# A macaron block's mixer woven by estimated engine clocks, with weight slots of its own for each dense stream and a full-array recurrence

## The chip, the core and the metric

The kernel runs on one core of a Trainium2 chip. Its time is the device time of one execution in microseconds; the lower the better. PE is the matrix engine (TensorE), DVE the vector engine, ACT the scalar engine, POOL the general engine (GpSimd), SP the engine that issues most transfers.

## What is computed

One layer of a hybrid model on 1024 tokens of width 1024, in float32: a gated feed-forward part (inner width 2816), a mixer, a second feed-forward part, and a small gated projection at the end. All the change is in the mixer:

```python
h = rms_norm(x, mix_norm)
z = h @ w_in
z_rwkv, z_attn, z_gate = jnp.split(z, [RWKV_COLS, RWKV_COLS + ATTN_COLS], axis=-1)
y_rwkv = rwkv7_time_mix(z_rwkv, ...)          # 8 heads of 64, below
y_attn = dilated_attention_mix(z_attn, ...)   # 3 groups of 4 heads, dilations 1, 4, 16
g_rwkv, g_attn = jnp.split(jax.nn.sigmoid(z_gate), N_BRANCHES, axis=-1)
merged = g_rwkv * (y_rwkv @ w_br_rwkv) + g_attn * (y_attn @ w_br_attn)
x = x + merged @ w_out
```

The recurrence of `rwkv7_time_mix`, per head, over the 1024 tokens:

```python
def step(state, inp):
    r_t, w_t, k_t, v_t, kk_t, a_t = inp
    sa = jnp.einsum('bhvk,bhk->bhv', state, -kk_t)
    state = (state * w_t[:, :, None, :] + sa[..., None] * (kk_t * a_t)[:, :, None, :]
             + v_t[..., None] * k_t[:, :, None, :])
    y_t = jnp.einsum('bhvk,bhk->bhv', state, r_t)
    return state, y_t
```

## The kernel before

**Products.** A dense float32 product is made of three faster ones: each operand is split into a high and a low part, and `mm3` issues high x high, high x low and low x high (lines 265 to 267). A weight chunk of 128 x 1024 comes by a transfer on SP into a staging slot `wst` (two of them, shared by all), ACT copies out the high part (L249), POOL subtracts for the low part (L250), and both lie in a slot `wsp` (a ring of three, shared by all). `wchunk` does all of this at the point where a block begins.

**The mixer's first part** (`rwkv`, L845 on). Two lora blocks come first (`zblock` for columns 12 and 13, run straight through). Then eight units, four blocks of two heads by two halves of the sequence, each through stages: `zstage` (three dense blocks of 24 matmuls of 128x512 each: the projections), `wkv_a` (scores, decay, and the inverse of a 16 x 16 corner by DVE steps), `wkv_b` (the rest of a triangular inverse in many matmuls of 64x32, then the recurrence over eight chunks of 64 tokens), and `wkv_c` (normalization of the result `yc` on DVE, ACT and POOL, its product with a gate, and four transposes of it on PE). A chunk of the recurrence is two half steps, each a pair of small float32 matmuls, one for each head, on quarters of the array, with a DVE step behind it (the matmuls are L1254 and L1263, the DVE steps L1258 and L1264):

```python
for h in range(2):
    hr = slice(64 * h, 64 * h + 64)
    PE.matmul(pu[ur[e], h, 256:320], lhsT=QR[hr, i, qs], rhs=S[hr, cc], start=True, stop=True)
...
A.activation(SP, S[:, cc], AF.Copy, scale=pcol)
V.tensor_tensor(out=UV[ur[e], i, e].rearrange("p (h s) -> p h s", h=2),
                in0=Ub[ur[e]].rearrange("p (h i) s -> p h i s", h=2)[:, :, i],
                in1=pu[ur[e], :, 256:320], op=ALU.subtract)
for h in range(2):
    hr = slice(64 * h, 64 * h + 64)
    PE.matmul(pu[hr, 0, 320:384], lhsT=BKn[:, i, e, hr], rhs=UV[:, i, e, hr], start=True, stop=True)
V.scalar_tensor_tensor(out=S[:, cc + 1], in0=pu[:, 0, 320:384], scalar=pcol, in1=SP, op0=ALU.mult,
                       op1=ALU.add)
```

**What sets the order.** Every engine takes its instructions in the order in which the program issues them, and waits at an instruction until what it needs is there. The stages are Python generators, and `weave` (L118) takes turns among them: B (`wkv_b`), C (`wkv_c`), A (`wkv_a`), and F, the dense streams: `zstage` and, as filler, the gate blocks of the merge and the first attention projections (`gates`, `qkv_first`). At each yield a stream says by hand how much PE time it just issued and how long it wants to wait (`yield 0.16, 0.5`; `yield 0, 8.0` in `wkv_c` ahead of the last product and the transposes; dense chunks `yield 0.65, 0, True`). `weave` keeps one clock from these numbers. A small stream whose wait is over goes first, in the order B, C, A; a dense chunk of three matmuls is issued if none is ready, after 2.0 us of small work in a row (BURST), or if the work of the last 3 us by this clock is under a threshold, in which small work counts a fraction.

**The second part.** Attention runs group by group: `attn_core` (scores, softmax, transposes of the probabilities, products), `qk_post` (norm and rotation of q and k), `qkv_gemm` (projections of the next groups), the rest of the filler gates, and `branch_r` (the recurrent branch's product), by the same `weave`. Then `attn_combine` joins the groups and `merge_a` and `out_early` make the merged result.

Of the kernel before, what the change touches and what calls it, by code (L numbers as in the profile page):

```python
# [18 lines left out]
P = 128  # L19
T = 1024  # L20
# [85 lines left out]

def later(cond, make):
    yield cond
    yield from make()


def weave(streams, until, burst=0.9):
# [7 lines left out]

    now, inside = 0.0, None
    wake = {id(e): 0.0 for e in streams}
    wait = {}
    hist = []

    def active(t0):
        return sum((min(e, now) - max(s, t0)) * r for s, e, r in hist if e > t0)

    small = 0.0
    while streams and not until():  # L130
# [3 lines left out]
        ok = [e for e in streams if id(e) not in wait and wake[id(e)] <= now]  # L134
        dense = [e for e in ok if e[0] == "F"]
        small_ok = [e for e in ok if e[0] != "F"]
        if inside is not None:
            dense = [inside]
        low = now > WIN and active(now - WIN) < ACT * WIN
# [4 lines left out]
        else:  # L144
            t = [wake[id(e)] for e in streams if id(e) not in wait]
            assert t, "every stream waits"
            now = max(now, min(t))
            small = 0.0
            continue
        try:  # L150
# [4 lines left out]
            continue  # L155
        if callable(r):
            wait[id(pick)] = r
            continue
        if r[0]:
            hist.append((now, now + r[0], 1.0 if pick[0] == "F" else r[3] if len(r) > 3 else 0.3))  # L160
            del hist[:-64]
        now += r[0]
        wake[id(pick)] = now + r[1]
        if pick[0] == "F":
            inside = pick if len(r) > 2 and r[2] else None
            small = 0.0
        else:
            small += r[0]


class K:
    def __init__(self, ctx, tc, a):
        self.ctx, self.tc, self.nc, self.a = ctx, tc, tc.nc, a
        self.n = 0
# [16 lines left out]
    def t(self, pool, shape, tag, dt=F32, bufs=None):  # L191
        kw = {} if bufs is None else {"bufs": bufs}
        return pool.tile(shape, dt, tag=tag, name=self.nm(tag), **kw)
# [58 lines left out]
    def wchunk(self, src, kdim, pool=None, tag="wsp", bufs=3):  # L252

        nc = self.nc
        n = kdim * src.shape[-1]
        st = self.t(self.wp, [P, 1024], "wst", bufs=2)
        nc.sync.dma_start(st[:, :n].rearrange("p (k n) -> p k n", k=kdim), src)
        sp = self.t(pool or self.wp, [P, 2, 1024], tag, dt=F32R, bufs=bufs)
        self.split(sp[:, :, :n], st[:, :n], lo_eng=nc.gpsimd)
# [92 lines left out]
    def forms_1(self, F, xn, gcol, fw, sp, pp):  # L352
# [8 lines left out]
        for q in range(4):  # L361
            g1, g2 = self.col(gcol, q), self.col(gcol, 4 + q)
            if q % 2 == 0:
                b12.append(self.t(self.wp, [P, 1024], "wst", bufs=2).rearrange("p (q f) -> p q f", q=2))
# [44 lines left out]
    def st_slot(self):  # L409
        return self.t(self.wp, [P, 2, 1024], "wsp", dt=F32R, bufs=3).rearrange("p s (c f) -> p s c f", c=2)  # L410
# [277 lines left out]
    def ffn_down(self, x, load_x, actD, wd, wr, hp, sp, pp, gcol, first, hT, hook, preload):  # L688
# [22 lines left out]
        def load_b(g, b):  # L711
# [12 lines left out]
            if g == 1:  # L724
                W = self.t(self.wp, [P, 1024], "wst", bufs=2).rearrange("p (q n) -> p q n", q=2)
# [1369 lines left out]
```

## Time and profile before

| what | us |
|---|---|
| runs | 2730.45, 2732.27, 2738.2 (median 2732.27) |
| profiled execution | 2731.04 |
| its span, first to last instruction | 2729.3 |
| PE busy | 2518.9 (92%) |
| DVE busy | 1586.2 (58%) |
| POOL busy | 1148.3 (42%) |
| ACT busy | 973.2 (36%) |

FFN1 takes the span up to about 781 us. The lora blocks and the eight units run to about 1429, attention to about 1792, the merge and the output product to 1840, and FFN2 and the last projection the rest. Tables by stretch give the busy time of each engine in it and the clock that was granted to PE, 1.00 for 2.4 GHz and 0.50 for 1.2 GHz; a value between is a mean over the two. In a timeline a matmul's length is from its start to its modelled end, and the next one starts before that; what one costs is read from the distance of two starts. A float32 matmul that isn't split leaves two records.

### The profile page before, as it was taken

Reading aid. Unit: us, or ns where it says so; the run is one execution under the profiler, and the core shown is the slowest. Engines: PE = TensorE matmul, PEld = TensorE weight load, DVE = VectorE, ACT = ScalarE, POOL = GpSimd, SP = SyncE. Lnnn points to the kernel's source line nnn. Section 1 sums busy time; section 2 is a strip of 40 time slices with the busy share of each in tenths; the row PEclk is TensorE's granted clock in tenths of the full one; section 3 lists DMA queues with packets and bytes.
Section 4 is the critical chain, followed back from the end, with each engine's and each line's share of the span. In section 5 each row is a group of like instructions: output and inputs, shape, how many; then the busy total and the mean of one; then the engine's idle time right before and its main releaser. Section 6 shows DMA issues by size and latency. Waiting matters only on the chain.

```text
span 2729.3 us, 37026 instructions
## 1 busy us (share of the span) xinstructions
PE 2518.9 (92%) x14541; PEld 2038.0 (75%) x14541; DVE 1586.2 (58%) x2519; ACT 973.2 (36%) x1700; POOL 1148.3 (42%) x635
## 2 busy tenths in 40 slices
PE   6899999899999999889989998879799999989899
PEld 5688888777777666667877998658578888768677
DVE  4865556788715555554356325382876556677852
ACT  5433333333434323332224343421533332333541
POOL 2675556555424333332222212150565655555540
PEclk9899999999999999999989999899899999999999
DMA  5222222736333222222231101572132222453532
GB/s 187 93 85 70 93 78 93 282 120 211 129 117 91 60 62 56 62 60 59 76 113 43 63 32 43 180 210 113 46 99 82 88 77 93 147 222 110 180 121 93
DMA packets 272498, 289.18 MB, mean 106 GB/s; under 512 B 46282, under 2 KB 202540, under 8 KB 272068
## 3 DMA queue, kind: packets, MB, share of 16 engines
q1 hardware_dynamic: 264932, 274.59, 30.7%
q10 hardware_dynamic: 7392, 12.23, 1.3%
q8 instruction: 114, 1.87, 0.3%
q14 instruction: 60, 0.49, 0.1%
HBM read 222.64 MB, written 64.14 MB: 105 GB/s over the span
## 4 chain that ended last, share of the span: by engine, by line
PE 48%; DVE 13%; POOL 3%; issue 2%; DMA 2%; ACT 2%; SPq 0%; ACTq 0%; DVEq 0%; POOLq 0%
PE g L265 7%; PE g L266 6%; PE g L267 6%; PE dn L266 6%; PE dn L267 6%; PE dn L265 5%; PE tr L267 1%; PE tr L265 1%; PE tr L266 1%; POOL wsp L250 1%; PE t L1055 1%; PE s L1575 1%; DMA fb<-f 1%; DVE sub L1119 1%; PE pt L1597 1%
## 5 line engine op out<-in xcount | busy, mean ns | idle before, releaser
L250 POOL TENSOR_TENSOR wsp<-wr,wsp 128x1024 fp32r<-128x1024 f32 (+1 forms) x158 | 361.5, 2296 | 374.4 <-ACT wsp L249 334.2
L250 POOL TENSOR_TENSOR wsp<-wst,wsp 128x1024 fp32r<-128x1024 f32 x71 | 173.4, 2445 | 425.2 <-ACT wsp L249 372.4
L250 POOL TENSOR_TENSOR wsp<-ws,wsp 128x1024 fp32r<-128x1024 f32 x88 | 222.0, 2524 | 212.0 <-ACT wsp L249 210.3
L265 PE MATMUL g<-h,wsp 128*128 128x512 f32 x496 | 220.7, 445 | 12.2 <-DVE h L1714 10.6
L265 PE MATMUL g<-wsp,h 128*128 128x256 f32 (+1 forms) x664 | 217.0, 327 | 16.0 <-ACT raw L1427 10.2
L267 PE MATMUL g<-wsp,h 128*128 128x256 f32 (+1 forms) x664 | 207.6, 313 | 0.0
L266 PE MATMUL g<-wsp,h 128*128 128x256 f32 (+1 forms) x664 | 207.5, 313 | 0.0
L267 PE MATMUL g<-h,wsp 128*128 128x512 f32 x496 | 201.3, 406 | 0.0
L266 PE MATMUL g<-h,wsp 128*128 128x512 f32 x496 | 201.0, 405 | 0.0
L407 DVE TENSOR_TENSOR ws<-wr 128x512 f32<-128x512 f32 x56 | 86.6, 1554 | 166.8 <-POOL x L250 165.4
L249 ACT ACTIVATE wsp<-ws 128x1024 fp32r<-128x1024 f32 (+1 forms) x110 | 106.4, 968 | 191.6 <-PE dn L267 74.4
L249 ACT ACTIVATE wsp<-wr 128x1024 fp32r<-128x1024 f32 (+1 forms) x158 | 133.7, 851 | 107.6 <-DVE wr L751 42.5
L265 PEld LDWEIGHTS g<-wsp,h 128*128 128x128 f32 x664 | 138.5, 209 | 28.2 <-ACT raw L1427 10.9
L265 PE MATMUL dn<-wsp,h 128*128 128x512 f32 x360 | 143.8, 405 | 13.5 <-DVE x L792 6.9
L266 PE MATMUL dn<-wsp,h 128*128 128x512 f32 x360 | 143.7, 399 | 7.9 <-POOL wsp L250 7.9
L267 PE MATMUL dn<-wsp,h 128*128 128x512 f32 x360 | 142.1, 396 | 0.7 <-DVE h L250 0.6
L266 PEld LDWEIGHTS g<-wsp,h 128*128 128x128 f32 x664 | 139.0, 209 | 3.7 <-issue 0.2
L267 PEld LDWEIGHTS g<-wsp,h 128*128 128x128 f32 x664 | 138.6, 209 | 3.7
L463 DVE TENSOR_TENSOR act<-act,m 128x512 f32<-128x512 f32 x88 | 130.7, 1485 | 1.4
L265 PEld LDWEIGHTS g<-h,wsp 128*128 128x128 f32 x496 | 96.5, 194 | 44.0 <-DVE h L1714 11.6
L267 PE MATMUL dn<-h,wsp 128*128 128x512 f32 x320 | 124.6, 389 | 0.0
L265 PE MATMUL dn<-h,wsp 128*128 128x512 f32 x320 | 124.5, 389 | 0.0
(467 smaller groups left out, 6604.6 us busy)
## 6 DMA issues: line engine op xcount, KB each, us to landing
wr<-ffn_w_down SPq DMA_DIRECT2D x44, 1024.0 KB
wst<-w_in SPq DMA_DIRECT2D x60, 512.0 KB
wr<-ffn_w_gate SPq DMA_DIRECT2D x44, 512.0 KB
wr<-ffn_w_up SPq DMA_DIRECT2D x44, 512.0 KB
actD<-act SPq DMA_DIRECT2D x44, 512.0 KB
a<-actD SPq DMA_DIRECT2D x12, 1024.0 KB
gate<-gst SPq DMA_DIRECT2D x26, 256.0 KB
wst<-ffn_w_down SPq DMA_DIRECT2D x10, 512.0 KB
```

The lines of the kernel that those rows point to most:

```text
L249: nc.scalar.activation(dst[:, 0], src, AF.Copy)
L250: (lo_eng or nc.vector).tensor_tensor(out=dst[:, 1], in0=src, in1=dst[:, 0].bitcast(F32), op=ALU.subtract)
L265: mm(ps, lhsT=l[0], rhs=r[0], start=first, stop=False)
L266: mm(ps, lhsT=l[0], rhs=r[1], start=False, stop=False)
L267: mm(ps, lhsT=l[1], rhs=r[0], start=False, stop=last)
L407: self.nc.vector.tensor_tensor(out=out, in0=R[:, i], in1=R[:, j], op=op)
L463: eng.tensor_tensor(out=a, in0=a, in1=v, op=ALU.mult)
L1055: PE.matmul(psd[h][:, i2, e].rearrange("p (a s) -> p a s", a=2), lhsT=BK[hr, i, 2 * e:2 * e + 2].rearrange("p a s -> p (a s)"), rhs=QR[hr, ...
L1119: V.tensor_tensor(out=pr[:, :s + 1, :n], in0=XT[:, :s + 1, s:s + 1].to_broadcast([64, s + 1, n]), in1=at[:, s:s + 1, s + 1:].to_broadcast( ...
L1575: PE.matmul(ps[h][:, pr, :nk * P], lhsT=qT[hr, pr, j * P:(j + 1) * P], rhs=kT[hr, pr, k0:k0 + nk * P], start=True, stop=True)
L1597: PE.transpose(pt[:, h], S[:, h, kt * P:(kt + 1) * P], self.ident)
```

## The change

There are four parts.

1. **Clocks.** A wrapper of each engine's calls keeps an estimated clock for PE, DVE, ACT, POOL and the transfers, from costs per instruction (DVE 0.155 us + 1.04 ns an element, ACT 0.18 + 0.84, POOL 0.15 + 2.2, a matmul by its columns, 0.095 for a change of array form, a transfer by its bytes and 2.2 us), and when each tile is ready. A stream now yields the tiles that its next step needs (`yield Need(yc)`), and `weave` compares their readiness with PE's estimated clock. The hand-written numbers are gone.
2. **Slots.** The ring of weight slots becomes three separate ones (`wsp0` to `wsp2`) with a new `wz`, the staging slots `wst0` and `wst1` belong to one dense stream each. `wload` (the transfer) and `wsplit` are called apart, a block ahead: `zstage` loads at a block's begin and splits three chunks into the block before. In attention the gates have a slot `wx`.
3. **Recurrence.** The two heads' states stand in the diagonal blocks of one 128 x 128 matrix `Sbd`, whose other blocks are zero. A half step is one float32 matmul on the full array instead of two on quarters; the state's DVE step becomes two of 64 x 64, ACT's scaled copy is 128 x 128 instead of 128 x 64.
4. **`wkv_c`** yields `Need(yc)` once more, between the last product and the transposes.

The instructions of the feed-forward parts stand in the same order as before.

```diff
+class Need:
+    def __init__(self, *tiles, more=None, late=0.0):
+        self.tiles, self.more, self.late = tiles, more, late
...
-def weave(streams, until, burst=0.9):
+def weave(c, streams, until, burst=0.9):
...
-        ok = [e for e in streams if id(e) not in wait and wake[id(e)] <= now]
+        now = c.at["PE"]
+        wake = {id(e): c.when(needs[id(e)].tiles) + needs[id(e)].late if id(e) in needs else 0.0 for e in streams}
+        ok = [e for e in streams if id(e) not in wait and wake[id(e)] <= now + 0.05]
...
-            hist.append((now, now + r[0], 1.0 if pick[0] == "F" else r[3] if len(r) > 3 else 0.3))
+            hist.append((now, c.at["PE"], 1.0 if pick[0] == "F" else 0.25))
...
@@ rwkv
+        Wl = self.wsplit(self.wload(a["w_in"][:, 12 * P:13 * P].rearrange("(k p) n -> p k n", p=P), KB, 0), sp, "wz", 1)
...
+        Sbd = [self.t(sp, [P, 9, P], f"Sbd{q}") for q in range(2)]
...
-        Wl, Wg = zw(12), zw(13)
+        Wg = self.wsplit(zload(13), None, 0)
...
-                W = zw(4 * x + hb)
+                if not zready:
+                    zsplit()
+                W = zready.pop()
+                if zorder:
+                    nextz.append(zload(zorder.pop(0)))
                 d = zt[x, hb, hf] = self.t(sp, [P, HALF], f"z{x}{hf}")
-                yield from zblock(4 * x + hb, W, hf, d)
+                for n, r in enumerate(zblock(4 * x + hb, W, hf, d)):
+                    yield r
+                    if n == 3 and nextz:
+                        zsplit()
...
@@ wkv_b
-                for h in range(2):
-                    hr = slice(64 * h, 64 * h + 64)
-                    PE.matmul(pu[ur[e], h, 256:320], lhsT=QR[hr, i, qs], rhs=S[hr, cc], start=True, stop=True)
-                yield 0.16, 0.5
-                SP = self.t(sp, [P, 64], "SP", bufs=2)
+                PE.matmul(U2, lhsT=QR[:, i, 0:2].rearrange("p a s -> p (a s)"), rhs=S[:, cc], start=True, stop=True)
+                yield Need()
+                SP = self.t(sp, [P, P], "SP", bufs=2)
...
+                yield Need(UV)
+                PE.matmul(dS, lhsT=BKn[:, i, e], rhs=UV[:, i, e], start=True, stop=True)
                 for h in range(2):
                     hr = slice(64 * h, 64 * h + 64)
-                    PE.matmul(pu[hr, 0, 320:384], lhsT=BKn[:, i, e, hr], rhs=UV[:, i, e, hr], start=True, stop=True)
-                V.scalar_tensor_tensor(out=S[:, cc + 1], in0=pu[:, 0, 320:384], scalar=pcol, in1=SP, op0=ALU.mult,
-                                       op1=ALU.add)
-                yield 0.16, 0.5
+                    V.scalar_tensor_tensor(out=S[hr, cc + 1, hr], in0=dS[hr, hr], scalar=pcol[hr], in1=SP[hr, hr],
+                                           op0=ALU.mult, op1=ALU.add)
+                yield Need(S)
...
@@ wkv_c
-        yield 0, 8.0
+        yield Need(yc, gs)
         V.tensor_tensor(out=yc, in0=yc, in1=gs, op=ALU.mult)
+        yield Need(yc)
         pst = self.t(pp, [P, HALF], "t1", bufs=4)
```

Three places in the order of the instructions. In all of them `g` is a PSUM bank of a dense block, `h` the normed input, `wsp` and `wz` weights; in the kernel after, every instruction has the line of the wrapper, L216. First PE in the recurrence of a unit, before (`st` is the bank of the recurrence, `S` the state):

```order
L1254 MATMUL st_7234<-S_7232,QR_6302 64x64 x2
L265 MATMUL g_7253<-h_792_4911,wsp_7249 128x512
L266 MATMUL g_7253<-h_792_4911,wsp_7249 128x512
L267 MATMUL g_7253<-h_792_4911,wsp_7249 128x512
L1263 MATMUL st_7234<-UV_6607,BKn_6583 64x64 x2
```

and after:

```order
L216 MATMUL st_8076<-Sbd_885_5616,QR_7066 128x128
L216 MATMUL g_8146<-h_858_5417,wsp_1261_7845 128x512 x3
L216 MATMUL st_8076<-UV_7326,BKn_7288 128x128
L216 MATMUL g_8146<-h_860_5428,wsp_1261_7845 128x512 x3
L216 MATMUL g_8146<-h_862_5439,wsp_1261_7845 128x512 x3
L216 MATMUL g_8146<-h_864_5450,wsp_1261_7845 128x512 x3
L216 MATMUL g_8146<-h_866_5461,wsp_1261_7845 128x512 x3
L216 MATMUL g_8146<-h_868_5472,wsp_1261_7845 128x512 x3
L216 MATMUL st_8076<-Sbd_885_5616,QR_7066 128x128
```

A pair on quarters became one full matmul, and between two of them stand three to fifteen dense matmuls where there were three.

Second PE around the transposes of `yc` (into `t_1241`, `t_1291`), before, between the first products of the next unit's inverse (L1182, then L1191 and L1193):

```order
L1182 MATMUL t_1236_7657<-TT_7504,SC_7040 64x32 x8
L1329 MATMUL t_1241_7689<-cst_p_66,yc_7463 128x128 x4
L1055 MATMUL t_1244_7698<-QR_7600,BK_7601 128x128
L1055 MATMUL t_1245_7699<-QR_7600,BK_7601 128x128
L1191 MATMUL t_1246_7702<-N_882_5609,TT_7504 64x32 x2
```

and after, between the end of that inverse (`t_1287`) and the next unit's recurrence (`Sbd`):

```order
L216 MATMUL t_1287_8051<-TT_7694,Qn_7779 64x64
L216 MATMUL g_8057<-h_784_4857,wsp_1261_7845 128x512 x3
L216 MATMUL g_8057<-h_788_4884,wsp_1261_7845 128x512 x3
L216 MATMUL g_8057<-h_792_4911,wsp_1261_7845 128x512 x3
L216 MATMUL t_1291_8084<-cst_p_66,yc_7688 128x128 x4
L216 MATMUL g_8057<-h_796_4938,wsp_1261_7845 128x512 x3
L216 MATMUL g_8057<-h_801_4967,wsp_1261_7845 128x512 x3
L216 MATMUL st_8076<-Sbd_885_5616,QR_7066 128x128
```

The transposes moved behind the next unit's whole inverse.

Third ACT at the start of the mixer, before (`ws` is the output of the last gates of FFN1; `h` the normed input; `zu` belongs to the first lora block):

```order
L1346 ACTIVATE ws_5368<-g_5369 128x512
L281 ACTIVATE h_853_5397<-dn_5398,pc_116 128x512
L281 ACTIVATE h_856_5409<-dn_5410,pc_116 128x512
L281 ACTIVATE h_858_5420<-dn_5421,pc_116 128x512
L249 ACTIVATE wsp_5797<-wst_5795 128x1024
```

and after:

```order
L216 ACTIVATE ws_5544<-g_5545 128x512
L216 ACTIVATE wz_5594<-wst_876_5592 128x1024
L216 DMA cst_r_5597<-cst_r 128x682
L216 DMA wl_5599<-rwkv_w 64x512
L216 DMA wl_5599<-rwkv_a 64x512
L216 DMA Qn_5623<-rwkv_g 128x512
L216 DMA gn_5798<-rwkv_gn_w 128x128
L216 DMA gn_5798<-rwkv_gn_b 128x128
L216 DMA gn_6251<-rwkv_gn_w 128x128
L216 ACTIVATE wsp_893_5628<-wst_892_5626 128x1024
L216 DMA gn_6251<-rwkv_gn_b 128x128
L216 ACTIVATE zu_5656<-g_5631,pc_116 128x512
```

The splits of the lora blocks' weights (`wsp_5619` and `wsp_5624` before, ahead of the piece shown) moved from among the FFN1 gates to behind the last of them (`ws_5544`).

Over the whole of the recurrent stage, changes between full and small array forms on PE fall from 478 to 160, counted up to the first transposes of attention. Five gate blocks (48 us of dense matmuls at full clock) that ran in attention's group 0 now stand in the last two units.

## Rows read from the trace of the kernel before

**Rows 1.** The page, busy time of PE (us, share of the span, instructions):

```profile
PE 2518.9 (92%) x14541; PEld 2038.0 (75%) x14541; DVE 1586.2 (58%) x2519; ACT 973.2 (36%) x1700; POOL 1148.3 (42%) x635
```

**Rows 2.** Windows: stretch, its length, busy time per engine, granted clock, DMA:

```profile
944.00:958.00 14.00, 11.66 (x88) 8.94 (x90) 3.94 (x6) 3.19 (x6) 4.45 (x3) 0.51 0.30 95
1320.00:1384.00 64.00, 64.00 (x813) 57.18 (x814) 20.42 (x72) 15.09 (x35) 10.92 (x8) 1.00 0.20 60
1384.00:1429.00 45.00, 32.76 (x175) 28.75 (x173) 29.11 (x46) 10.82 (x16) 18.71 (x10) 0.89 0.49 159
795.00:1429.00 634.00, 576.53 (x5396) 442.17 (x5396) 319.42 (x748) 199.10 (x397) 203.91 (x160) 0.94 0.26 73
1441.00:1513.00 72.00, 66.79 (x418) 48.67 (x418) 42.06 (x126) 34.29 (x95) 16.55 (x7) 0.93 0.14 45
1513.00:1573.00 60.00, 60.00 (x376) 57.12 (x372) 20.68 (x34) 15.84 (x28) 15.65 (x6) 1.00 0.20 67
1429.00:1792.00 363.00, 335.90 (x2164) 290.14 (x2165) 168.12 (x450) 138.92 (x355) 77.67 (x31) 0.94 0.24 78
```

**Rows 3.** PE's waits, 795 to 1429: total us, times, longest:

```profile
PE t L1329 <- DVE yc L1326: 24.0, 7, 7.2
PE g L265 <- ACT raw L1427: 10.2, 2, 5.5
PE t L1055 <- ACT wsp L249: 6.2, 2, 3.3
PE t L1182 <- DMA TT<-tD: 3.4, 1, 3.4
...
PE t L914 <- POOL BK L911: 2.4, 1, 2.4
```

**Rows 4.** Timeline of PE in a recurrence: start, length, line, tile, shape:

```profile
973.17 0.33 PE L1254 MATMUL st<-S,QR 64*64 64x64 f32 x4
...
973.77 0.40 PE L266 MATMUL g<-h,wsp 128*128 128x512 f32 x1
974.00 0.40 PE L267 MATMUL g<-h,wsp 128*128 128x512 f32 x1
974.33 0.34 PE L1263 MATMUL st<-UV,BKn 128*64 128x64 f32 x4
```

**Rows 5.** Timeline of PE, unsplit float32 matmuls on the full array:

```profile
795.09 3.70 PE L914 MATMUL t<-Qn,BK 128*128 128x512 f32 x8
...
971.13 0.95 PE L1108 MATMUL t<-rki,kk 128*128 128x2 f32 x8
```

**Rows 6.** Groups of DVE, 795 to 1425: busy, mean ns, idle before:

```profile
L1258 DVE TENSOR_TENSOR UV<-Ub,st 64x128 f32<-64x128 f32 x64 | 18.2, 285 | 62.1 <-PE st L1254 61.6
L1264 DVE SCALAR_TENSOR_TENSOR S<-st,PC,SP 128x64 f32<-128x64 f32 x64 | 18.1, 283 | 42.1 <-PE st L1263 42.0
```

**Rows 7.** Timelines of SP, ACT and POOL, one weight chunk:

```profile
757.60 0.37 SPq L257 DMA_DIRECT2D wst<-w_in  x1
...
762.36 1.06 ACT L249 ACTIVATE wsp<-wst 128x1024 fp32r<-128x1024 f32 x1 [3.21 <-DMA wst<-w_in]
...
763.50 2.40 POOL L250 TENSOR_TENSOR wsp<-wst,wsp 128x1024 fp32r<-128x1024 f32 x1 [3.57 <-ACT wsp L249]
```

**Rows 8.** Timeline of DVE, begin and end of the last unit's `wkv_c`:

```profile
1383.75 0.76 DVE L1302 TENSOR_REDUCE gst<-st 128x4 f32<-128x256 f32 x2 [2.26 <-PE st L1278]
...
1398.89 2.83 DVE L1326 TENSOR_TENSOR yc<-yc,gsl 128x512 f32<-128x512 f32 x1 [4.13 <-POOL yc L1324]
```

**Rows 9.** PE's waits, 1429 to 1792:

```profile
PE g L265 <- DVE h L1714: 10.6, 2, 9.9
```

**Rows 10.** Attention's group 0: two steps on DVE, dense filler on PE:

```profile
1499.72 0.42 DVE L1579 CUSTOM_DVE_ANT_0 S<-s,cst_a 128x256 f32<-128x256 f32 x1 [0.87 <-PE s L1575]
...
1506.07 0.42 DVE L1579 CUSTOM_DVE_ANT_0 S<-s,cst_a 128x256 f32<-128x256 f32 x1 [1.10 <-PE s L1575]
...
L265 PE MATMUL g<-h,wsp 128*128 128x512 f32 x36 | 16.4, 456 | 0.0
```

More of the change, by code (lines that the diff above doesn't have):

```diff
@@ L107, in later, with __init__ @@
+class NC:
+    def __init__(self, nc):
+        self._nc, self.clocks = nc, Clocks()
+        for n, e in (("tensor", "PE"), ("vector", "DVE"), ("scalar", "ACT"), ("gpsimd", "POOL"), ("sync", "SP")):
+            setattr(self, n, Engine(getattr(nc, n), e, self.clocks))
+class Need:
+    def __init__(self, *tiles, more=None, late=0.0):
+        self.tiles, self.more, self.late = tiles, more, late
 def later(cond, make):
@@ L137, in weave @@
         if inside is not None:
-            dense = [inside]
-        low = now > WIN and active(now - WIN) < ACT * WIN
+            dense = [inside] if inside in dense else []
+        low = active(now - WIN, now) < ACT * WIN
         if dense and (small > burst or low or not small_ok):
@@ L144, in weave @@
         else:
-            t = [wake[id(e)] for e in streams if id(e) not in wait]
+            t = [wake[id(e)] for e in streams if id(e) not in wait and (inside is None or e[0] != "F" or e is inside)]
             assert t, "every stream waits"
-            now = max(now, min(t))
+            c.at["PE"] = max(now + 0.02, min(t))
             small = 0.0
@@ L1445, in qkv_gemm, with get @@
+        free = [0, 1, 2]
+        def get():
+            nonlocal raw
+            q = free.pop(0)
+            W = self.wsplit(raw, None, q)
+            raw = load()
+            return W, q
+        raw = load()
+        nxt = [get(), get()]
+        for g, x in jobs:
+            cur, nxt = nxt, []
+            W = [w for w, q in cur]
+            if x < 2:
                 yield lambda: g == 1 and x == 0 or ("post", g - 1 + x, 1 - x, 1) in done
-                W = self.qkv_weights(g, x)
@@ L1472, in qkv_gemm @@
+            free.extend(q for w, q in cur)
+            if raw:
+                nxt.append(get())
         done.add("gemm")
@@ L1875, in mixer @@
         done = set()
-        gates = self.gates(hT, mx, D_["gate"], range(gates0, 16))
+        self.gslots = [(None, 1), (None, 2)]
         def fill():
-            yield from take(gates, max(NFIRST - gates0, 0) * 16)
-            yield from self.qkv_first(hT, mx, D_["raw"])
+            yield from self.fill(hT, mx, D_["gate"], D_["raw"], range(gates0, NFIRST))
             done.add("raw0")
-            yield from gates
+            yield from self.gates(hT, mx, D_["gate"], range(NFIRST, 16))
             done.add("gates")
@@ L1896, in mixer @@
             env = dict(done=done, raw={}, qk={}, v={}, mx=mx)
[L1897 removed]
+            weave(nc.clocks, filler, lambda: "raw0" in done)
             vt = self.t(sp1, [P, NT, 256], "vt", bufs=2)
```

432 lines of the change are left out of this document (296 added, 136 removed).

## The prediction

> **What bounds the kernel now.** I read the page's busy table first: PE is busy 2518.9 us of a 2729.3 us span [rows 1], so some 210 us is all that waits can give back; the rest has to come from cheaper work or a faster clock. The orders of FFN1, FFN2 and the last stage agree on every engine before and after, so all is decided between 781 and 1792 us. The table of windows [rows 2] shows two parts. In the recurrent stage (795 to 1429) PE is busy 576.53 of 634 us: 57.5 idle, and a granted clock of 0.94. In attention (1429 to 1792) it is 335.90 of 363: 27 idle, clock again 0.94. A clock mean of 0.94 between the levels 1.2 and 2.4 GHz means that 12% of the stretch ran at half speed, 76 us in the first part. The window 944 to 958 is one such stretch: clock 0.51, PE busy 11.66 of 14. The unit at 1320 to 1384 shows the other end: 64.00 busy of 64, clock 1.00.
>
> The list of PE's waits [rows 3] says what the idle time is: 24.0 us in seven waits of the `yc` transposes (L1329) for DVE, 10.2 of the last dense blocks for `raw`, 6.2 of the score matmuls behind a weight split on ACT. The timeline of the recurrence [rows 4] shows a cost that is no wait: with clock and supply full, three dense matmuls start 0.23 us apart, but from the first small matmul (973.17) to the next (974.33) is 1.16 us, where 3 x 0.227 = 0.68 is dense. So 0.475 us goes on one small pair with its change of array form there and back.
>
> **The change part by part**, against the profiled execution (span 2729.3, 1.74 outside it: 2731.04; the median of the runs, 2732.27, lies 1.2 above).
>
> *Recurrence.* 8 units x 16 half steps = 128 pairs become one 128x128 f32 matmul each, in the array form of the dense work. The price of one: the eight records of L1108 start within 0.95 us, by their spacing 0.11 us a record and two records a matmul, 0.22 us [rows 5]. That matmul moves 2 columns, so 128 columns may cost more; but the transposes and L914's 512 columns (3.70 us for 8 records, two a matmul) scale to 0.43/4 x 2 = 0.215 at 128 [rows 5]. I take 0.22: 128 x (0.475 - 0.22) = **-32 us**. Ends: -32, and 0 if the wider work waits as long as it saves. Beside it the DVE update becomes two of 64x64 for one of 128x64 (0.28 us each, [rows 6]) and the ACT copy twice as wide. Both hide while PE has dense matmuls to fill: DVE sat idle 61.6 and 42.0 us ahead of these two lines waiting for PE, 64 times each, some 1.0 and 0.65 us a time [rows 6]; a second update of 0.28 fits in that. Without this cover it is 64 x 0.28 = 18 us.
>
> What the trace shows of the forms is that a form change is dear [rows 4]. The Trainium skill, TensorEngine Tiling (Array Packing), Theoretical Speedup, promises up to 2x or 4x from splitting the array for operands of at most 64, and its Key Properties say that independent tiles run in parallel; this speaks against giving up the two packed tiles. Key Properties also say that a change of mode drains the array. By the first rule alone the full form would double the price of a pair and the term would be a loss; the row of 0.475 us an island agrees with the second.
>
> *Other form changes.* Outside the recurrence the count of full-to-small changes up to the first attention transposes falls by 62, from 478 to 160 in all (256 are the recurrence's). Two changes make one island; the surplus there is 0.475 less the small pair itself (0.27 to the next dense start), so 0.2 an island: 31 x 0.2 = **-6** (0 to -6).
>
> *`yc` transposes.* They stood ahead of the first inverse matmuls of the next unit, with the DVE multiply not yet done; now they stand behind the whole inverse and three to four dense chunks, some 20 us later. Six or seven of the waits go: **-22** (-24 to -12). The last unit has no next inverse to stand behind. Its chain from the last recurrence result (1383.75) to the end of the multiply (1398.89 + 2.83) takes 18 us [rows 8]; the order now puts only some 8.6 us of dense work there, where before there were 16.5: a new wait of 9 against the old 1.5, **+8** (0 to +10).
>
> *Clock.* Each long `yc` wait is followed by half speed: 944 to 958 after the wait that ended at 946, and so in units 1 to 6; unit 7 without the wait keeps 1.00 [rows 2]. 11.66 us of work at half speed is 5.8 lost in 14; of the 76 us at half speed the tail holds 2 x 0.11 x 45 = 10 [rows 2], so 66/14 x 5.8 = 27 is the stake. The inverse stretches are still poor in dense matmuls, and the recurrence now takes about 21 us of dense work a unit for 10 before, so they become poorer. I take **-18** (0 to -27).
>
> *Head-of-line waits.* The score matmuls waited 6.2 us for ACT to finish a weight split queued ahead of their evictions [rows 3]. Splits now stand a block ahead: **-6** (0 to -9).
>
> *Tail of the stage.* The last attention blocks waited 10.2 us for `raw` slots [rows 3], with the clock at 0.89 [rows 2]. The gates that came later now come here: **-5** (-15 to +5).
>
> *Start of the stage.* Before, both first weight chunks were split while the last FFN1 gates ran (load 757.60, ACT 762.36, POOL 763.50 to 765.90, [rows 7]): 4.8 us from issue to ACT, 3.5 for the split. Now the first split stands behind the last gate's activation on ACT, and each next load waits until POOL has read the one slot. Behind that activation of some 0.6: 0.6 + 3.5, so 4 us of wait; the second: load and split 8.3 against a block of 24 x 0.227 = 5.5 us, 2.7; the third likewise behind an ACT activation, 3: 9.7, less the 2.4 that the `BK` wait (L914) cost there before [rows 3]: **+7** (0 to +12). Queued behind the split on ACT are only the loads of constants.
>
> *New in-order waits.* PE takes its queue in order; where an estimate is short, it stands. The nearest row is the one wait of 3.4 us for `TT`, which came in one unit of eight [rows 3]. I take **+12** (0 to +30), 1.5 us a unit: between nothing and that wait in each unit (27), nearer to what most units show.
>
> *Attention.* 48 us of gate blocks move from group 0 into units 6 and 7; as work this is neutral. Group 0 (1441 to 1513, PE 66.79 of 72, [rows 2]) loses its filler: 36 matmuls of 0.227 at each of three lines alone are 24.5 us [rows 10]. What remains is a chain of 6.35 us a step (1499.72 to 1506.07, [rows 10]); eight steps are 51 us for 72 - 24.5 = 47 that would be left, and with the transposes before them and a clock that may fall I take **+15** (0 to +36). Against this the rwkv branch's matmuls now lie beside group 2's core, where PE waited 10.6 us for the combine's `h` [rows 9], and 0.06 x 363 = 22 us of clock time is missing in this part [rows 2]: **-25** (-45 to 0).
>
> Sum: -32 - 6 - 22 + 8 - 18 - 6 - 5 + 7 + 12 + 15 - 25 = -72. 2731 - 72 = 2659; with the 1.2 to the median **2660 us**.
>
> **The rivals.**
> *The clock still falls in the inverse stretches* (it follows poor supply, not the wait): for it, the stretches have less dense work than before; against it, unit 7 with such a stretch at 1.00. The -18 is gone and some more half speed comes: 2660 + 18 + 8 = 2686.
> *Attention starves*: group 0 at +36 in place of +15 and the overlap giving 5 in place of 25: 2660 + 21 + 20 = 2701. For it: the 6.35 us step and only some 7 us of filler left; against it: with full supply group 1 ran at 1.00 without idle time (1513 to 1573, [rows 2]).
> *The weaving doesn't do what it says*: estimated clocks drift from the real ones, new waits equal those removed, and only the recurrence pays: 2732 - 32 = 2700; at half that, 2716.
> *Slower*: one mechanism, PE's in-order queue. Each unit has about 26 places where PE depends on a result just made (16 half steps, 6 inverse steps, 4 more), 208 in all. The chain between half steps is now longer (two narrow updates, the inverse's DVE steps of the next unit queued between them, a copy twice as wide). The other terms gain 72 + 12 = 84; a mean wait of 84/208 = 0.40 us at each place eats that, and above 0.45 the kernel is slower: at 0.55 it is 208 x 0.55 = 114, so 2732 - 84 + 114 = 2762. Against it: DVE's idle time waiting for PE at just these places [rows 6].
>
> **How the numbers follow.** About 0.3% (8 us) is what a measurement can tell from no change. Forecast (2635 to 2682) 0.42; better still, with clock, head-of-line and overlap terms near their lower ends, 0.05; clock rival (2682 to 2697) 0.17; starving (2690 to 2715) 0.10; doesn't do what it says 0.10, of which 0.06 below 2724 and 0.04 within 8 us of no change; slower mechanism 0.16, of which 0.03 within. Faster 0.42 + 0.05 + 0.17 + 0.10 + 0.06 = 0.80, same 0.07, slower 0.13. The lower end takes the forecast with the clock at -27, the tail at -15, no new waits and the overlap at -45: 2660 - 9 - 10 - 12 - 20 = 2609; the upper reaches through the rivals short of no change, 2730.
>
> **What the profile after would show.** Right: no PE wait for `yc` in units 0 to 6 and one of about 9 us in the last; the half step with full-form matmuls 0.22 apart from its dense neighbours; granted clock 1.00 in most windows of the units; 3 waits for `wz`/`wsp` at 781 to 815. Wrong: clock 0.90 still in units 1 to 6 (first rival); group 0 of attention with PE below 0.8 busy (second); long lists of short PE waits for `UV`, `Sbd`, `TT` (slower). The forecast fails as a whole if the 128x128 f32 matmul costs clearly more than 0.22 us between dense ones.

## The result: slower, and the profile after

The changed kernel takes 2747.64 us (median of seven runs) for 2732.27 before, a ratio of 1.0069 with an interval of 1.0053 to 1.0085. The forecast was 2660. So the sign was wrong, and by a size (88 us) that no single mis-sized term explains.

The page's busy line of the changed kernel answers to [rows 1]; PE is busy 10 us longer, in a span that is 16 us longer:

```profile
PE 2528.6 (92%) x14285; PEld 2065.8 (75%) x14285; DVE 1614.8 (59%) x2583; ACT 978.2 (36%) x1700; POOL 1138.4 (41%) x637
```

I cut both traces at the same places: the last FFN1 gate matmul, the first lora matmul of unit 0, the first transpose of attention, the first and last matmul of the merge. Idle is PE's, half speed is the time at a granted clock of 0.5, in us:

| stretch | before: length, idle, half speed | after: length, idle, half speed |
|---|---|---|
| FFN1 | 781.1, 56.2, 37.5 | 782.7, 54.7, 44.4 |
| start of the mixer | 48.0, 2.5, 0 | 70.1, 7.2, 13.7 |
| eight units | 600.1, 55.2, 78.7 | 617.7, 48.3, 95.6 |
| attention | 362.8, 26.9, 40.8 | 332.3, 40.9, 51.6 |
| merge | 47.3, 13.7, 3.4 | 56.2, 11.9, 23.5 |
| rest | 890.0, 55.9, 51.0 | 886.0, 53.3, 48.3 |

The start and the units together grew by 39.7 us. Some 48 us of dense work moved into them from attention. By count it is 168 matmuls of the gates, which is three and a half blocks and not five, and 81 half-wide ones of the first attention projections. So on equal work the start and the units gained 8, where the forecast's terms for them summed to -62. Attention and the merge shrank by 21.6, so on equal work they lost 26, where the forecast had -10. FFN1 and the rest, whose order is the same, gave 2.4 back. -8 + 26 - 2 = 16, the difference of the spans.

The windows of the changed kernel (columns as in [rows 2]) show that the clock did not recover, 0.92 in the units, and fell in the start, around the end of attention and in the merge:

```profile
783.00:853.00 70.00, 63.06 (x234) 46.26 (x235) 5.99 (x10) 21.57 (x36) 20.50 (x20) 0.90 0.35 107
853.00:1471.00 618.00, 569.73 (x5222) 467.56 (x5223) 330.20 (x834) 197.30 (x385) 195.02 (x153) 0.92 0.26 72
1771.00:1803.00 32.00, 15.40 (x69) 12.46 (x67) 14.28 (x22) 5.74 (x7) 8.30 (x4) 0.78 0.77 238
1803.00:1859.00 56.00, 44.06 (x143) 31.18 (x144) 46.27 (x51) 16.94 (x24) 28.55 (x15) 0.79 0.67 212
```

PE's waits from 783 to 1471 answer to [rows 3]. The `yc` transposes wait 4.0 us, once, for 24.0; the score matmuls no longer wait for a split. In their place stand waits that were short before or not there:

```profile
PE t L216 <- DVE TT L216: 11.6, 4, 6.7
PE st L216 <- DVE UV L216: 6.6, 6, 2.2
PE t L216 <- DVE BK L216: 6.3, 3, 3.3
PE g L216 <- ACT raw L216: 5.8, 2, 5.2
PE g L216 <- DVE z L216: 4.8, 1, 4.8
PE st L216 <- DVE Sbd L216: 4.6, 5, 1.3
...
PE t L216 <- DVE yc L216: 4.0, 1, 4.0
```

The longest of them shows where `yc` went. First DVE's timeline, then PE's, of the changed kernel:

```profile
1337.76 0.69 DVE L216 TENSOR_TENSOR yc<-yc,grsy 128x512 f32<-128x512 f32 x1
1342.50 0.69 DVE L216 TENSOR_TENSOR yc<-yc,gsl 128x512 f32<-128x512 f32 x1 [4.05 <-POOL yc L216]
1343.11 0.75 DVE L216 TENSOR_TENSOR TT<-TT,t 128x256 f32<-128x256 f32 x2
```

```profile
1344.00 0.76 PE L216 MATMUL t<-QR,BK 64*128 64x128 f32 x2 [6.71 <-DVE TT L216]
```

DVE stood 4 us at the last product of `yc` for POOL's three steps, and the update of `TT`, for which PE's next score matmuls waited, was queued behind it. DVE had waited there before too (19.6 us in six waits; 29.8 in eight now). What is new is that something PE needs stands behind that wait.

The recurrence came near its price in the best places. This row group answers to [rows 4]: from one full matmul to the next is 1403.80 - 1402.87 = 0.93 us with three dense ones between, for 1.16 before. It is among the shortest: the 38 such half steps at full clock and without idle time take 0.92 to 1.19 us, 1.00 in the mean.

```profile
1402.87 0.39 PE L216 MATMUL st<-Sbd,QR 128*128 128x128 f32 x2
1403.02 0.94 PE L216 MATMUL g<-h,wsp 128*128 128x512 f32 x3
1403.80 0.38 PE L216 MATMUL st<-UV,BKn 128*128 128x128 f32 x2
```

### The profile page after: what moved, and what is told of

Same layout as the page of the kernel before. It is cut to its first block, busy times and chain, and to the rows that moved or that the text cites. A ratio compares the mean times of both kernels' runs of the same rounds, so it can differ in the third digit from the quotient of the medians.

```text
span 2745.0 us, 36570 instructions
## 1 busy us (share of the span) xinstructions
PE 2528.6 (92%) x14285; PEld 2065.8 (75%) x14285; DVE 1614.8 (59%) x2583; ACT 978.2 (36%) x1700; POOL 1138.4 (41%) x637
## 4 chain that ended last, share of the span: by engine, by line
PE 64%; DVE 20%; issue 5%; POOL 4%; ACT 3%; DMA 3%; SPq 0%; ACTq 0%; DVEq 0%; POOLq 0%
PE dn L216 24%; PE g L216 24%; PE tr L216 8%; PE t L216 4%; DVE ws L216 2%; POOL wsp L216 2%; DVE h L216 2%; DVE rt L216 1%; DVE wr L216 1%; PE st L216 1%; PE pt L216 1%; DMA wr<-ffn_w_down 1%; PE s L216 1%; POOL yc L216 1%; DVE x L216 1%
## 5 line engine op out<-in xcount | busy, mean ns | idle before, releaser
L216 POOL TENSOR_TENSOR wsp<-wr,wsp 128x1024 fp32r<-128x1024 f32 (+1 forms) x158 | 355.2, 2257 | 383.3 <-ACT wsp L216 327.3
L216 DVE TENSOR_TENSOR ws<-wr 128x1024 f32<-128x1024 f32 (+1 forms) x136 | 196.8, 1454 | 271.1 <-POOL x L216 165.5
L216 PE MATMUL g<-wsp,h 128*128 128x256 f32 (+1 forms) x1992 | 325.4, 316 | 20.7 <-DVE m L216 8.2
L216 PE MATMUL g<-h,wsp 128*128 128x512 f32 x1200 | 327.9, 416 | 7.9 <-POOL wsp L216 4.6
L216 PEld LDWEIGHTS g<-wsp,h 128*128 128x128 f32 x1992 | 290.3, 208 | 39.2 <-DVE m L216 9.0
L216 POOL TENSOR_TENSOR wsp<-ws,wsp 128x1024 fp32r<-128x1024 f32 x88 | 222.0, 2525 | 211.9 <-ACT wsp L216 210.2
L216 POOL TENSOR_TENSOR wsp<-wst,wsp 128x1024 fp32r<-128x1024 f32 x58 | 139.4, 2406 | 395.5 <-ACT wsp L216 325.8
L216 PE MATMUL dn<-wsp,h 128*128 128x512 f32 x1080 | 273.2, 407 | 17.4 <-POOL wsp L216 8.5
L216 PE MATMUL dn<-h,wsp 128*128 128x512 f32 x1056 | 260.4, 395 | 9.4 <-ACT h L216 5.0
L216 PEld LDWEIGHTS g<-h,wsp 128*128 128x128 f32 x1200 | 222.5, 195 | 57.5 <-POOL wsp L216 6.6
L216 PEld LDWEIGHTS dn<-wsp,h 128*128 128x128 f32 x1080 | 210.9, 197 | 69.9 <-POOL wsp L216 11.0
L216 PE MATMUL tr<-h,wsp 128*128 128x512 f32 x1008 | 242.3, 390 | 0.1
L216 PEld LDWEIGHTS dn<-h,wsp 128*128 128x128 f32 x1056 | 200.0, 190 | 52.4 <-ACT h L216 5.4
L216 PEld LDWEIGHTS tr<-h,wsp 128*128 128x128 f32 x1008 | 189.2, 188 | 39.7 <-DVE h L216 0.5
L216 PE MATMUL dn<-wsp 128*128 128x512 f32 x792 | 191.9, 399 | 8.8 <-POOL wsp L216 6.4
L216 PEld LDWEIGHTS dn<-wsp 128*128 128x128 f32 x792 | 148.6, 191 | 45.0 <-POOL wsp L216 11.1
L216 ACT ACTIVATE wsp<-ws 128x1024 fp32r<-128x1024 f32 (+1 forms) x110 | 106.4, 968 | 193.7 <-PE dn L216 78.7
L216 ACT ACTIVATE wsp<-wr 128x1024 fp32r<-128x1024 f32 (+1 forms) x158 | 133.8, 852 | 116.6 <-DVE wr L216 51.1
L216 PE MATMUL g<-f,wsp 128*128 128x512 f32 x576 | 142.1, 398 | 7.9 <-ACT ntb L216 7.6
L216 PE MATMUL dn<-f,wsp 128*128 128x512 f32 x528 | 130.3, 395 | 12.8 <-ACT f L216 7.1
L216 PEld LDWEIGHTS g<-f,wsp 128*128 128x128 f32 x576 | 111.0, 193 | 32.3 <-ACT ntb L216 8.1
L216 DVE TENSOR_TENSOR act<-act,m 128x512 f32<-128x512 f32 x88 | 129.7, 1473 | 1.4
```

The lines of the kernel that those rows point to most:

```text
L216: return call(*args, **kw)
```

## The experiments

Theories: **A**, half speed follows the long `yc` wait; **B**, it comes with stretches that have little dense work; **C**, attention starves without its gates; **D**, a chain through DVE, ACT and POOL at each unit's boundary, and not PE's work, sets the length of a unit; **E**, the recurrence is bound by DVE; **F**, the combine at the end of attention lost the work that had covered it.

**The recurrence alone.** In the kernel before, only the full-array form with its two narrow DVE updates. To make room, this kernel and the three of the shorter chain built on the kernel before also have a smaller scratch buffer for transfers; the changed kernel has it too, and its effect was not measured by itself.

```diff
-                for h in range(2):
-                    hr = slice(64 * h, 64 * h + 64)
-                    PE.matmul(pu[ur[e], h, 256:320], lhsT=QR[hr, i, qs], rhs=S[hr, cc], start=True, stop=True)
+                PE.matmul(U2, lhsT=QR[:, i, 0:2].rearrange("p a s -> p (a s)"), rhs=S[:, cc], start=True, stop=True)
...
+                PE.matmul(dS, lhsT=BKn[:, i, e], rhs=UV[:, i, e], start=True, stop=True)
```

> The kernel before with the full-array recurrence alone (block-diagonal state, one 128x128 matmul per half step, two DVE updates); the old weave, slots and transposes stay. Only the unused transfer scratch is made smaller to fit the second state. Theory 1 (the recurrence pays as in the changed kernel's trace, where a half step of three dense and one full matmul takes 0.93 us for 1.16 before): 128 x 0.23 = 29 us, so 2732 - 29 = 2703. Rival (one chunk of three dense matmuls is too short a cover for two DVE updates): PE waits for Sbd and UV of 0.1 to 0.3 us at most half steps, 2715 to 2740.

2741.47 us for 2733.12 before, ratio 1.0025 (1.0015 to 1.0036): slower, above both expectations. The units took 604.6 us for 600.1, and PE's waits from 785 to 1438 say why:

```profile
PE t L1329 <- DVE yc L1326: 37.9, 7, 7.9
...
PE st L1261 <- DVE UV L1258: 7.0, 4, 2.1
...
PE st L1254 <- DVE Sbd L1264: 4.0, 4, 1.7
```

The `yc` wait grew by 14 us and those inside the recurrence by 6; half speed rose from 79 to 99 us. PE's work, counted at full clock (busy time less half of what ran at half speed), fell by 17 us; idle time rose by 14 (69.5 for 55.2), and the clock took 7. The saved work came back as waiting, most of it outside the recurrence. That is against the prediction's step and gave theory D.

**The transposes later.** In the kernel before, longer waits of the C stream:

```diff
-        yield 0, 8.0
+        yield 0, 16.0
         V.tensor_tensor(out=yc, in0=yc, in1=gs, op=ALU.mult)
+        yield 0, 3.0
```

> The kernel before with longer hand-written waits of the C stream (16 for 8 us ahead of the last product, 3 more ahead of the transposes), so that the yc transposes stand behind the first part of the next unit's inverse. Theory A (half speed follows the long yc wait): the waits of 24 us fall to under 5 and the half-speed stretches of units 1 to 6 with them, clock of 795 to 1429 from 0.94 to above 0.97, 2732 - 20 - 25 = 2687. Theory B (half speed comes with stretches that have little dense work, wait or no wait): the waits fall, the clock of the stage stays at 0.93 to 0.95, about 2712.

2752.18, ratio 1.0065 (1.0044 to 1.0085): slower, as neither theory had it. No `yc` wait is left, but the scores now wait for DVE, and the units' clock stays at 0.93:

```profile
PE t L1055 <- DVE BK L1028: 20.9, 5, 6.9
```

With 5.5 us for the other half of `BK` (L1030) that is more than the 24 us that went: the products on DVE had moved with the transposes, among the steps that the scores need. Theory A falls as it was put: half speed stayed (87 us for 79) without the wait it was to follow. That another long wait does the same is not excluded, since those for `BK` came in its place.

**Dense work spread.** In the changed kernel, two numbers of `weave`:

```diff
-ACT = 0.45
+ACT = .65
...
-            hist.append((now, c.at["PE"], 1.0 if pick[0] == "F" else 0.25))
+            hist.append((now, c.at["PE"], 1.0 if pick[0] == "F" else .1))
```

> The changed kernel with two numbers of its weaving: the share of recent dense work under which a dense chunk goes first raised from 0.45 to 0.65, and small work counted at 0.1 for 0.25. Dense chunks are spread more evenly over scores and inverse. Theory B (poor supply drops the clock, and the change moved the supply from the inverse into the recurrence): clock of the recurrent stage rises from 0.92 to 0.95 or more, half-speed work of 102 us falls by a third or more, 2747 - 15 to 20 = about 2730. Theory A (waits drop the clock): no difference beyond 5 us, 2742 to 2752.

2783.53, ratio to before 1.0185 (1.017 to 1.02): 36 us slower than the changed kernel, and outside both expectations. The units took 647.9 us, idle 83.9, clock 0.91. PE's waits grew: `BK` 17.7, `yc` 16.8, `Sbd` 13.6. So theory B did not get its test, since the waits came with the spread. That more dense chunks ahead of the small steps delayed them is the likely reading; no run tests it.

**Gates held back.** In the changed kernel, one line:

```diff
             done.add("raw0")
+            yield lambda: "y" in D_
```

> The changed kernel with gates 11 to 15 held back until attention begins. Theory C (attention lost because its filler was used up in units 6 and 7): group 0 and the combine are covered again, attention to the first merge matmul loses its surplus of some 18 us over before and the wait of 16.6 us for ya shrinks; units 6 and 7 are shorter by the 48 us of gates plus what they then lack in cover: about 2730. Rival (units 6 and 7 without filler run at half speed and wait): the gain is given back there, 2745 to 2765.

2795.58, ratio to before 1.0235 (1.0213 to 1.0257), above both expectations. Here are the windows of the last two units, first the changed kernel, then this one:

```profile
1270.00:1471.00 201.00, 180.49 (x1841) 150.14 (x1840) 108.99 (x291) 59.26 (x115) 56.59 (x40) 0.92 0.26 80
```

```profile
1280.00:1471.00 191.00, 131.64 (x1513) 113.58 (x1513) 100.74 (x264) 44.92 (x94) 46.38 (x36) 0.72 0.20 58
```

With some 60 us of dense matmuls less ahead of attention (240 of the gates and 48 half-wide ones), the two units shrank by some 10: PE idled 59 us and ran at 0.72. In attention and the merge the 60 us then cost 56 (444.4 for 388.5). So theory C is worth little: the score matmuls' waits for `ast`, a buffer of DVE's softmax, fell from 10.7 to 3.0 us, but the gates hid only some 4 us of what they cost, and the wait for `ya` stayed (16.8). And it is the first sign that PE's work does not set the units' length.

**A shorter chain at the unit's boundary.** In the kernel before, in the changed one, and in the one with the recurrence alone. POOL prepares the factors while DVE is still at the inverse root, and DVE ends without a wait for POOL:

```diff
+        G.tensor_tensor(out=i4(yb), in0=i4(yb), in1=gn[:, 1:2].to_broadcast([P, 4, P]), op=ALU.add)
+        G.tensor_tensor(out=yb, in0=yb, in1=gs, op=ALU.mult)
+        G.tensor_tensor(out=i4(gs), in0=i4(gs), in1=gn[:, 0:1].to_broadcast([P, 4, P]), op=ALU.mult)
...
         V.tensor_tensor(out=hs_(yc), in0=hs_(yc), in1=bc(rs_), op=ALU.mult)
-        G.tensor_tensor(out=i4(yc), in0=i4(yc), in1=gn[:, 0:1].to_broadcast([P, 4, P]), op=ALU.mult)
-        G.tensor_tensor(out=i4(yc), in0=i4(yc), in1=gn[:, 1:2].to_broadcast([P, 4, P]), op=ALU.add)
...
-        G.tensor_tensor(out=yc, in0=yc, in1=sq, op=ALU.add)
+        V.tensor_tensor(out=yc, in0=yc, in1=gs, op=ALU.mult)
+        V.tensor_tensor(out=yc, in0=yc, in1=yb, op=ALU.add)
         yield 0, 8.0
-        V.tensor_tensor(out=yc, in0=yc, in1=gs, op=ALU.mult)
```

That is the edit of the kernel before. Besides the shorter chain, the last product now stands ahead of the 8 us wait, so that the transposes come later behind it; the run tests the two together.

> The kernel before with a shorter wkv_c: POOL works out bonus, bias and gate factors while DVE does the inverse root, and after it three DVE steps follow without a wait for POOL (in place of one DVE step, three of POOL at 1.28 us and one of DVE behind them). PE's work and order are the same but for the place of the transposes. Theory D (at a unit's boundary a chain through DVE, ACT and POOL of some 25 us, not PE's work, sets the length of the unit): the yc waits fall from 24 us to under 10, part of the half speed with them, 2733 - 20 to 40, about 2705. Rival (PE's work is the bound, as the prediction had it, and the yc wait is PE's only loss there): waits go elsewhere or fall by at most 10 us, 2723 to 2733.

2724.84, ratio 0.9977 (0.9968 to 0.9986): less than D asked, and in the rival's range. The time from the first `gst` step to the last DVE step of `yc`, summed over the eight units, fell from 148 to 101 us, and the kernel gained some 7. The `yc` waits went, but two of the scores for ACT (15.0 us) came, and half speed stayed at 73.5 us. So a us off this chain is not a us gained either: another wait takes over.

> The changed kernel with the same shorter wkv_c. Theory D, and that DVE's own in-order wait for POOL (4 us at the yc product, with the update of TT queued behind it) took the place of PE's wait: PE's waits for TT (11.6 us) fall under 5, those of 1.3 us and more ahead of the scores go, half-speed work falls, 2747 - 15 to 30, about 2725. Rival: TT and BK waits stay, since DVE has simply too much to do at the boundary: 2740 to 2750.

2718.98, ratio to before 0.9955 (0.9943 to 0.9968); that is 29 us under the changed kernel's 2747.64, measured in another set of runs. As expected, the waits for `TT` are gone from PE's list, and DVE's for POOL at `yc` from its own; those for `BK` stayed (5.9 us). The units shrank from 617.7 to 589.1 us, with half speed at 67.7 for 95.6. Of these 29 us some 13 are dense work that the new order left to attention, which with the merge took no longer (388.3 us for 388.5). This fits that DVE's wait for POOL was the cost of the new place of `yc`, but the run doesn't part it from the new order. What then leads the list is the recurrence's own wait:

```profile
PE st L216 <- DVE UV L216: 12.8, 8, 3.8
```

> The kernel before with the full-array recurrence and the shorter wkv_c together. Theory D: with a shorter chain the recurrence's saving on PE (it was 8 us slower alone, with yc waits of 37.9) is no longer eaten, so this beats the shorter chain alone by 10 to 25 us: about 2690. Rival E (the recurrence itself is bound by DVE, which has the next unit's inverse queued between the two narrow updates): equal to the shorter chain alone within 5 us or slower.

2705.07, ratio 0.9908 (0.9887 to 0.9928), faster than both kernels. The same recurrence that cost 8 us alone now brings 20 against the shorter chain alone (2724.84), within D's 10 to 25, though the time itself is above the 2690 that was expected. E falls. D holds in this: once the long waits of the chain are gone, PE work that is saved is time that is saved. The units take 569.4 us, and PE's first wait is

```profile
PE t L1331 <- DVE yc L1327: 11.7, 5, 3.6
```

**A longer chain.** The other way round, in the kernel before: two POOL steps more, which multiply `yc` by one:

```diff
         G.tensor_tensor(out=yc, in0=yc, in1=sq, op=ALU.add)
+        for _ in range(2):
+            G.tensor_scalar(out=yc, in0=yc, scalar1=1.0, scalar2=None, op0=ALU.mult)
```

> The kernel before with two more POOL steps on yc (a multiply by one, 0.62 us each by L911's row) in the middle of wkv_c's chain; PE's work and order unchanged. Theory D (the chain at the unit's boundary is on the path): each of eight units longer by about 1.25 us, 2732 + 10 = 2742. Rival (PE's work is the bound, the yc wait small change): 2732 to 2735.

2766.02, ratio 1.0123 (1.0103 to 1.0144), above both expectations. A step took 1.49 us where I had 0.62, as POOL's timeline shows for the two together:

```profile
1091.87 3.06 POOL L1326 TENSOR_SCALAR yc<-yc 128x512 f32<-128x512 f32 x2
```

So eight units got 24 us more of these two steps, and the kernel took 34 more. The units grew by 28 (628.3 for 600.1), and the time from `gst` to the end of `yc` by 39 (187 for 148), so the steps also delayed others. The longer wait is in one line, for 24.0 before:

```profile
PE t L1331 <- DVE yc L1328: 57.8, 7, 10.4
```

**Less work for PE.** In the kernel before, the third product of the units' projections is left out, so the output loses accuracy:

```diff
+                    nc.tensor.matmul(ps, lhsT=W[:, 0, kb], rhs=rh, start=kb == 0, stop=False)
+                    nc.tensor.matmul(ps, lhsT=W[:, 1, kb], rhs=rh, start=False, stop=kb == KB - 1)
```

> The kernel before with the third product (weights high, input low) left out in the 48 half blocks of the recurrent stage's projections: 384 matmuls less of 0.227 us each, 87 us of work if all of them are gone from PE's path, spread over all units, with no change of any other engine's work (the output loses accuracy). If PE's work is the bound, as the prediction had it: 2732 - 87 = 2645, or 2660 with some new waits. Theory D: the units shrink by much less, a third of it or so, and PE's waits and half-speed stretches take the rest: 2690 to 2715.

The expectation counted twice too many: there are 24 half blocks, 192 matmuls, 43.5 us. 2725.53, ratio 0.9983 (0.9967 to 0.9999): some 5 us of 43.5, outside both expectations. The window of the units shows where the rest went, 80 us idle for 55 and a clock of 0.88 for 0.93 (the profile is of the slowest of its ten runs, 2737.08):

```profile
828.00:1435.00 607.00, 526.77 (x5107) 405.75 (x5104) 310.99 (x747) 186.71 (x375) 192.41 (x152) 0.88 0.25 71
```

```profile
PE t L1334 <- DVE yc L1331: 42.4, 7, 10.6
```

So PE's work is not the bound of the units. In this profile the rest came back in two halves: 25 us as idle time, and some 25 because 109 us of PE's work ran at half speed, for 59 before. That the chain alone holds the units is not shown by it.

**The later transposes, with the short chain.** In the fastest kernel, the wait ahead of the transposes:

```diff
-        yield 0, 8.0
+        yield 0, 11.0
```

> The kernel of the shorter chain with the full-array recurrence, and the wait ahead of the yc transposes 11 us in place of 8: they stand behind the first part of the inverse, where the last three DVE steps have been issued already. Theory D: PE's 11.7 us of yc waits go and nothing stands in DVE's queue for them, 2705 - 8 to 15, about 2693. Rival (the waits move to the scores behind them, as with the late transposes alone): 2700 to 2710.

2708.51, ratio 0.9918 (0.9904 to 0.9933), the same as without. The `yc` waits went, those for `BK` came (7.8 and 2.4 us): the rival.

**The branch's second half held.** In the changed kernel, half of `branch_r` waits for group 2's core:

```diff
+            if b == 4:
+                yield hold
```

> The changed kernel with the second half of branch_r held until group 2's core is done, so that 98 dense matmuls in place of 69 stand between the last product of attention and the first merge matmul (130 before). Theory F (the combine's chain lost its cover to group 2): the wait for ya falls from 16.6 us to about 10 and the half speed of 23 us in the merge with it; less what group 2 loses: 2747 - 8 = 2739. Rival (group 2's core needs that cover as much): its waits grow by what ya's falls, 2745 to 2750.

2744.8, ratio to before 1.0059 (1.0033 to 1.0086), no clear difference from the changed kernel. The longest wait for `ya` fell from 16.6 to 13.7 us, the waits for `h` took that (4.3 for 1.5), and the merge kept its 23 us at half speed. So this much of the branch does not bear out F; more of it was not tested. What attention and the merge lost stays partly open.

## Why the prediction was wrong, step by step

**The step that failed is the first:** that PE's busy share of 92% and its list of waits bound the recurrent stage, so that each us of PE work or wait removed is a us gained. In its place the runs showed that PE work taken off comes back as idle time and half speed: 43.5 us left out gave some 5, and the recurrence alone took 17 us off PE and cost 8. The chain of the kernel before at one boundary, from the view that follows the last released instruction back, would have shown it. It leaves PE at 1054.75, near the end of a recurrence, and returns 29 us later (lines left out are more of the same on DVE and POOL):

```profile
1054.46 0.29 PE st L1263 x4
1054.85 0.28 DVE S L1264
...
1061.45 0.67 DVE gst L1302 x2
...
1063.14 0.64 ACT ysq L1310
...
1070.83 2.30 DVE grsu L241
...
1074.34 1.26 POOL yc L1319
...
1080.67 1.75 DVE yc L1326
1082.42 0.67 DVE z L888
1083.31 0.49 ACT Qn L1159
1083.85 1.28 PE t L1055 x4
```

In these 29 us PE runs work that is not on the chain; from there to the next such place, at 1118.41, the chain runs on PE itself for most of 35 us. PE's work can be less without moving the end by as much, as the 43.5 us left out (5 gained) and the 60 us held back (10) show, while 24 us more chain cost 34. The other way the chain is no price list: shortened by 47 us it gave 7, since other waits took over.

The Trainium skill, Perfetto Trace Analysis, Identifying the Most-Contended Engine, says to optimize the engine with the highest occupancy first; for TensorE it takes the matmul busy share for a poor measure of how near a kernel is to roofline, and looks at the weight loads' share beside the throughput. Here the matmul share (92%) and the weight loads' (75%) both stand above DVE's 58%, and in the units the runs decide against going by them: 43.5 us less work on PE gave some 5.

The balance of the start and the units on equal work shows the size of each miss. PE's work, counted at full clock, fell by 27 us (forecast 38, the recurrence and the other form changes). The clock took back 21 (forecast: 18 gained). Idle time fell by 2 (forecast 6, all terms of waits together). So of the 54 us missed there, the clock is 39. Most of the work was saved, and half speed took most of it back. The other 36 us of the 88 are attention's, below.

*Recurrence (-32).* The price was mis-sized. The 84 half steps at full clock and without idle time cost 0.31 us beyond their dense matmuls (0.227 each), for 0.48 before, where the forecast had 0.22: 128 x 0.17 is 21 us of PE work saved, not 32. What lay "on the path" was wrong too: +8 alone, -20 once the chain was shorter. The cover argument failed as well. DVE's idle time ahead of these lines [rows 6] was an average; `UV` and `Sbd` waits came to 11.2 us in the changed kernel, for 4.6 at these places before.

*`yc` (-22, +8 in the last unit).* The waits went as forecast, 24.0 to 4.0, and the last unit's was 4.0, not 9. What was missed is that the order moved on DVE as well: its own wait for POOL held `TT`. The term for new in-order waits (+12) should have carried that. `TT`, `UV`, `BK`, `z` and `Sbd` together are 33.9 us, for some 13 in the list before, so +21.

*Clock (-18).* It went the other way, as the first rival had it, and further. By the distances of starts, PE spent 102 us of work at half speed from the mixer's start to attention, for 60 before, so about (102 - 60)/2 = +21. Two runs speak for poor supply as its cause. With the same idle time in the units (81 and 80 us), the longer chain had 66 us of PE's work at half speed, and the run with work left out 109. That the changed kernel's clock fell because dense matmuls went from the inverse into the recurrence is argued from the order; the run that was to test it did not. Of the prediction's cause, the long `yc` wait, it was shown only that half speed does not need it.

*Head-of-line (-6), tail (-5).* Right: the wait of 6.2 is gone, that for `raw` fell from 10.2 to 5.8.

*Start (+7).* Waits of 7.2 us for 2.5, so +4.7, right in kind; but 13.7 us at half speed came with them, which the term did not have.

*Attention (-10).* +26 with the merge. Idle time is 12 us more: 17.4 us of waits for `ya` stand where 10.6 for `h` stood, and the score matmuls wait 10.7 us for `ast`, for 3.5 before. PE's work at half speed is 47 us for 37, so 5 more are lost, all of it in the merge (20 us for 3); the other half-speed time that came on top was idle. Another 3 us only changed sides: 14 output matmuls that stood behind the merge stand ahead of its end now. Some 6 us are not placed. The cause I gave, a starved group 0, is the 7 us for `ast` at most: with the gates held back these waits went, and attention and the merge gained only 4.

The mechanism of the slower rival, PE's queue meeting waits at every dependent place, is not what happened: PE's idle time in the units fell (48.3 for 55.2). Two rivals were near. The clock rival had the direction, but 26 us for a miss of 39. "The weaving doesn't do what it says, waits take the place of waits" was right on the waits, with a wrong floor: it assumed that the recurrence would still pay in time.

## What to carry to other kernels

A busy engine need not be the bound where the chain of dependent steps leaves it: look at the chain across one period of the loop before pricing work on the busiest engine, and test it by adding a step to the chain and by leaving work out of the engine. When a wait is moved out of one engine's queue, follow the instruction that was waited for through its own engine's queue, and see what now stands behind it there. Here the shorter chain had to come first: the edit that only saved work on the filled engine cost 8 us by itself and brought 20 after it.

## What the runs showed of the hardware

The same DVE step on 128 x 8 elements took 0.17 us and, beside a POOL weight split, 2.37. First DVE, then POOL, in the kernel before:

```profile
1068.55 0.17 DVE L241 TENSOR_TENSOR grsu<-grsy 128x8 f32<-128x8 f32 x1
...
1070.76 2.37 DVE L241 TENSOR_TENSOR grsu<-grsy 128x8 f32<-128x8 f32 x1
```

```profile
1070.65 2.44 POOL L250 TENSOR_TENSOR wsp<-wst,wsp 128x1024 fp32r<-128x1024 f32 x1 [0.59 <-ACT wsp L249]
```

It ends when the split ends (1073.13 and 1073.09). The Trainium skill, SBUF — State Buffer, SBUF: two separate sides, says that VectorE with two SBUF inputs and GpSimd hold a shared port pair for a whole instruction and the loser waits; the trace agrees, and the wait falls on the chain. And less work for PE went with a lower clock: 43.5 us less of it came with 72 us more at half speed in the profiled run, and in all ten runs the mean granted clock was 0.946 to 0.954, where the kernel before had 0.959 to 0.962.
